# The first load of a half-rotary kernel in two transfers by partitions, 16 and 112

## The chip, the cores and the metric

The kernel runs on one core of a Trainium2 chip. Its time is the device time of one execution in microseconds (us), as the median of several runs; beside it stands one profiled execution, whose trace is read here. Of the core's engines only VectorE (DVE in the profile) computes. SyncE (SP) and GpSimd (POOL) issue transfers between the chip's memory (DRAM) and the on-chip memory, which has 128 partitions; sixteen DMA engines carry them out.

## The reference

`x` is 16 x 512 x 16 x 64 (batch, sequence, heads, dim), `cos` and `sin` are 512 x 32. Only the first half of the last axis is rotated, in two quarters of 16 elements; the second half, `x2`, is passed on.

```python
half_dim = dim // 2
x1, x2 = (x[..., :half_dim].copy(), x[..., half_dim:].copy())
cos = cos[None, :, None, :].copy()
sin = sin[None, :, None, :].copy()
rotated_first = x1[..., :half_dim // 2] * cos[..., :half_dim // 2] - x1[..., half_dim // 2:] * sin[..., :half_dim // 2]
rotated_second = x1[..., :half_dim // 2] * sin[..., :half_dim // 2] + x1[..., half_dim // 2:] * cos[..., :half_dim // 2]
return np.concatenate([rotated_first, rotated_second, x2], axis=-1).astype(np.float32)
```

## The kernel before

The 8192 positions (batch times sequence) are cut into T = 4 tiles of 128 partitions by K = 16 consecutive positions. One position is 16 heads x 64 floats, so a partition's row of a tile is 64 KB in one contiguous piece of DRAM, and a tile is 8.39 MB. The tiles live in `ring`, which has NS = 3 slots: tile 3 takes the slot of tile 0. A tile is loaded, rotated in place, and stored from the same bytes, so that the second half of each vector needs no work.

Two helpers issue the large transfers: `load(t, lo, hi)` on SP's queue (line 55) and `store(t, lo, hi, queue)`, on SP's queue unless told otherwise (line 58). A transfer moves positions lo to hi of all 128 partitions of a tile; the first half of a tile (0 to KC = 8) is 32 KB a partition.

`cos` and `sin` go by two small transfers on GpSimd's queue (lines 63 and 64) into every fourth partition of `stage`. VectorE spreads them over all partitions with a shuffle (line 73), four copies into `packed` (line 80) and four into `table` (line 83).

`rotate(t, lo, hi)` is four VectorE instructions over positions lo to hi of a tile: two products, the first into `b_t` in the accumulation memory (line 96) and the second in place (line 97), a difference (line 98) and a sum (line 101).

The order of the work is the order in the code on each engine's queue. SP issues load(0), load(1), load(2, 0, KC), then store(0) when tile 0 is rotated, the second half of load(2), load(3) when store(0) has landed (it needs the slot), store(1), and store(3) at the end; store(2) goes by GpSimd's queue. A dependency written out by hand (lines 118 to 123) holds store(1) back until positions 8 to 13 of tile 2 are rotated.

Any instruction that reads what a transfer wrote waits for that transfer's completion. The first `rotate(0, 0, KC)` reads all 128 partitions of slot 0.

Of the kernel before, what the change touches and what calls it, by code (L numbers as in the profile page):

```python
# [1 line left out]

# [4 lines left out]


@with_exitstack
def kernel(  # L10
    ctx: ExitStack,
    tc: tile.TileContext,
    x: bass.AP,
    cos: bass.AP,
    sin: bass.AP,
    out: bass.AP,
):
    nc = tc.nc
    fp32 = mybir.dt.float32
    P = 128  # L20
    B, S, H, D = x.shape
    Q = D // 4
    HF = D // 2

    K = 16
    T = B * S // (P * K)
    PB = S // K
    REP = P // PB  # L30
    R = H * D
    NS = 3
    KC = K // 2
    KM = 13

    xf = x.rearrange("b s h d -> (b s h d)").rearrange("(t p f) -> t p f", t=T, p=P)
    of = out.rearrange("b s h d -> (b s h d)").rearrange("(t p f) -> t p f", t=T, p=P)
    cosf = cos.rearrange("(p k) j -> p (k j)", k=K)
    sinf = sin.rearrange("(p k) j -> p (k j)", k=K)

    const_pool = ctx.enter_context(tc.tile_pool(name="const", bufs=1))
    b_pool = ctx.enter_context(tc.tile_pool(name="bp", bufs=1, space=bass.MemoryType.PSUM))


    ring = const_pool.tile([P, NS, K, H, D], fp32)
    stage = const_pool.tile([P, 2, K, HF], fp32)
    spun = const_pool.tile([P, 2 * K, Q], fp32)
    packed = const_pool.tile([PB, 2 * K, Q], fp32)
    table = const_pool.tile([P, 2, K, 2, Q], fp32)

    def rows(t, lo, hi):
        return ring[:, t % NS, lo:hi].rearrange("p k h d -> p (k h d)")

    def load(t, lo=0, hi=K):
        return nc.sync.dma_start(out=rows(t, lo, hi), in_=xf[t, :, lo * R : hi * R])

    def store(t, lo=0, hi=K, queue=nc.sync):
        return queue.dma_start(out=of[t, :, lo * R : hi * R], in_=rows(t, lo, hi))  # L58


    nc.vector.memset(stage[:, :, :, 0:Q], 0.0)  # L61
    spread = stage.rearrange("(j b) t k i -> j b t (k i)", b=REP)
    nc.gpsimd.dma_start(out=spread[:, 0, 0], in_=cosf)  # L63
    nc.gpsimd.dma_start(out=spread[:, 0, 1], in_=sinf)  # L64
    load(0)
    load(1)
    load(2, 0, KC)

    PQ = PB // REP
    nc.vector.stream_shuffle(  # L73
        out=spun[:],
        in_=stage.rearrange("p t k j -> p (t k) j")[:, :, 0:Q],
        mask=[j % PQ * REP for j in range(PB)],
    )
    for q in reversed(range(REP)):
        n = PQ * (q + 1)
        nc.vector.tensor_copy(out=packed[0:n], in_=spun[q * PB : q * PB + n])  # L80

    for r in range(REP):
        nc.vector.tensor_copy(  # L83
            out=table[r * PB : (r + 1) * PB].rearrange("p t k c j -> p (t k) c j"),
            in_=packed.unsqueeze(2).to_broadcast((PB, 2 * K, 2, Q)),
        )
    C = table[:, 0].rearrange("p k c j -> p k (c j)")
    Sn = table[:, 1].rearrange("p k c j -> p k (c j)")

    def rotate(t, lo, hi):  # L90
        x1 = ring[:, t % NS, lo:hi, :, 0:HF]
        c = C[:, lo:hi].unsqueeze(2).to_broadcast((P, hi - lo, H, HF))
        s = Sn[:, lo:hi].unsqueeze(2).to_broadcast((P, hi - lo, H, HF))
        b_full = b_pool.tile([P, KC, H, HF], fp32, name="b_t")
        b_t = b_full[:, 0 : hi - lo]
        nc.vector.tensor_mul(out=b_t, in0=x1, in1=s)  # L96
        nc.vector.tensor_mul(out=x1, in0=x1, in1=c)  # L97
        nc.vector.tensor_sub(  # L98
            out=x1[:, :, :, 0:Q], in0=x1[:, :, :, 0:Q], in1=b_t[:, :, :, Q:HF]
        )  # L100
        return nc.vector.tensor_add(  # L101
            out=x1[:, :, :, Q:HF], in0=x1[:, :, :, Q:HF], in1=b_t[:, :, :, 0:Q]
        )

    rotate(0, 0, KC)
    rotate(0, KC, K)
    store(0)
    load(2, KC, K)
    load(3)
    rotate(1, 0, KC)  # L110
    rotate(1, KC, K)
    behind_loads = store(1)
    rotate(2, 0, KC)
    near = rotate(2, KC, KM)
    rotate(2, KM, K)
    store(2, queue=nc.gpsimd)

    tc.add_manual_dep(
        behind_loads.ins,
        near.ins.name,  # L120
        mybir.DependencyInfo(mybir.DependencyClass.Sync, mybir.DependencyReason.DATA),
        reason="the store follows the loads at the DMA engines",
    )
    rotate(3, 0, KC)
    rotate(3, KC, K)
    store(3)


# [1 line left out]
_INS = ['x', 'cos', 'sin']  # L130
_OUTS = [((16, 512, 16, 64), 'float32')]


# [23 lines left out]
```

## Time and profile before

| | |
|---|---|
| median of 3 runs | 161.42 us (161.4 to 161.52) |
| profiled execution, span from first to last instruction | 159.5 us |
| VectorE busy | 112.9 us |
| bytes read and written in DRAM | 33.69 MB and 33.55 MB |
| mean rate over the span | 422 GB/s |
| load(0), load(1), load(2, 0, KC) issued | from 0.74 us, 1.33 us for the three |
| first `rotate` starts | 22.99 us |
| last `rotate` ends, store(3) issued | 131.2 us |

The span is shorter than the time of a run by 1.9 us, which lie around the instructions. The profile shows the instructions of each engine and, apart from them, the packets of the DMA engines. The instruction that issues a transfer is short (0.34 to 0.64 us here); the transfer lands much later, and the profile gives the time from issue to landing on its own. "q1" is the queue that SP's transfers use, "q0" that of GpSimd's.

Two views matter most below. The strip of the span in 40 slices shows which engine is busy when:

```profile
DVE  1000959999999999999999999999999990000000
POOL 3000000000000000000000000010000000000000
DMA  7969979899699699699996996996996996998966
```

Each digit is the busy share of a slice of 4 us in tenths. VectorE is idle for the first 16 us but for a little, and again behind 131 us; the DMA digits go up and down because a packet is booked in one slice and a full row lasts more than half of one.

The other is the waits of SP's queue, which say what the issue of a transfer stood for:

```profile
SPq L58 <- DVE ring L101: 84.1, 3, 30.5
SPq L152 <- DMA out_dram<-ring: 26.8, 2, 14.4
SPq L58 <- DMA ring<-in_x_dram: 22.3, 2, 20.8
SPq L55 <- DMA out_dram<-ring: 21.0, 1, 21.0
```

The columns are the waiting line and what it waited for, then the total in us, the number of times and the longest. The last row is load(3), which waits 21 us for store(0) to leave its slot.

### The profile page before, as it was taken

The numbers are of one execution on the slowest core, as the hardware profiler recorded it, in microseconds if no ns is written. First come the engines' busy times: TensorE is split into PE (matmuls) and PEld (weight loads), VectorE is DVE, ScalarE is ACT, GpSimd is POOL, SyncE is SP. The second block draws the span as 40 slices with busy tenths as digits, with TensorE's granted clock in tenths as the row PEclk, the third lists the DMA queues.
The fourth block names the chain that finished last, engine by engine and source line by source line (L and its number), as shares of the span: only waits on it lengthen the run. The fifth ranks groups of instructions, "written<-read, shape, count | busy, mean of one in ns | idle before, by whom it ended". The sixth has DMA issues, their size and how long they took to land.

```text
span 159.5 us, 115 instructions
## 1 busy us (share of the span) xinstructions
DVE 112.9 (71%) x47; POOL 1.9 (1%) x7
## 2 busy tenths in 40 slices
DVE  1000959999999999999999999999999990000000
POOL 3000000000000000000000000010000000000000
DMA  7969979899699699699996996996996996998966
GB/s 263 542 263 542 444 345 526 362 427 526 271 493 551 263 526 526 263 395 427 493 526 263 526 526 263 526 526 263 526 526 263 526 510 279 526 427 362 526 263 263
DMA packets 1360, 67.24 MB, mean 422 GB/s; under 512 B 176, under 2 KB 176, under 8 KB 208
## 3 DMA queue, kind: packets, MB, share of 16 engines
q1 hardware_dynamic: 1152, 58.72, 85.7%
q0 software_dynamic: 208, 8.52, 12.4%
HBM read 33.69 MB, written 33.55 MB: 422 GB/s over the span
## 4 chain that ended last, share of the span: by engine, by line
DVE 61%; DMA 14%; issue 5%; DVEq 1%
DVE b_t L96 22%; DVE ring L97 22%; DMA ring<-in_x_dram 14%; DVE ring L101 10%; DVE ring L98 7%; DVEq L152 1%; DVEq L96 0%
## 5 line engine op out<-in xcount | busy, mean ns | idle before, releaser
L96 DVE TENSOR_TENSOR b_t<-ring,table 128x4096 f32<-128x4096 f32 (+2 forms) x9 | 35.6, 3959 | 2.1 <-DMA ring<-in_x_dram 1.9
L97 DVE TENSOR_TENSOR ring<-ring,table 128x4096 f32<-128x4096 f32 (+2 forms) x9 | 35.6, 3950 | 0.3
L98 DVE TENSOR_TENSOR ring<-ring,b_t 128x2048 f32<-128x2048 f32 (+2 forms) x9 | 18.4, 2050 | 0.3
L101 DVE TENSOR_TENSOR ring<-ring,b_t 128x2048 f32<-128x2048 f32 (+2 forms) x9 | 18.4, 2043 | 0.0
L73 DVE LOAD_MASK_SELECT spun<-stage x1 | 0.0, 14 | 14.4 <-DMA stage<-in_sin_dram 14.4
L83 DVE COPY table<-packed 32x1024 f32<-32x1024 f32 x4 | 2.7, 684 | 0.1
L58 POOL DMA_DIRECT2D out_dram<-ring x1 | 0.6, 559 | 101.7 <-DVE ring L101 101.7
L80 DVE COPY packed<-spun 32x512 f32<-32x512 f32 (+3 forms) x4 | 1.7, 416 | 0.1
L61 DVE MEMSET stage<- 128x512 f32 x1 | 0.5, 485 | 0.9 <-PEq L141 0.9
L73 DVE STREAM_SHUFFLE spun<-stage 128x512 f32<-128x512 f32 x1 | 0.7, 722 | 0.0
L63 POOL DMA_DIRECT2D stage<-in_cos_dram x1 | 0.6, 642 | 1.3 <-DVE stage L61 1.3
L64 POOL DMA_DIRECT2D stage<-in_sin_dram x1 | 0.5, 532 | 0.0
L141 POOL MEMSET const-bfloat16-1.0<- 128x1 bf16 x1 | 0.1, 101 | 0.0
L141 POOL MEMSET const-float32-0.0<- 128x1 f32 x1 | 0.1, 98 | 0.2 <-issue 0.2
L141 POOL MEMSET const-float32-1.0<- 128x1 f32 x1 | 0.1, 98 | 0.0
L141 POOL MEMSET const-uint8-127<- 128x1 uint8 x1 | 0.1, 98 | 0.0
## 6 DMA issues: line engine op xcount, KB each, us to landing
ring<-in_x_dram SPq DMA_DIRECT2D x2, 4096.0 KB, 40.7
stage<-in_cos_dram POOLq DMA_DIRECT2D x1, 64.0 KB, 8.9
stage<-in_sin_dram POOLq DMA_DIRECT2D x1, 64.0 KB, 13.3
ring<-in_x_dram SPq DMA_DIRECT2D x3, 28.9
out_dram<-ring SPq DMA_DIRECT2D x3, 27.4
out_dram<-ring POOLq DMA_DIRECT2D x1, 39.5
```

The source lines that it names most:

```text
L58: return queue.dma_start(out=of[t, :, lo * R : hi * R], in_=rows(t, lo, hi))
L61: nc.vector.memset(stage[:, :, :, 0:Q], 0.0)
L63: nc.gpsimd.dma_start(out=spread[:, 0, 0], in_=cosf)
L64: nc.gpsimd.dma_start(out=spread[:, 0, 1], in_=sinf)
L73: nc.vector.stream_shuffle(out=spun[:], in_=stage.rearrange("p t k j -> p (t k) j")[:, :, 0:Q], mask=[j % PQ * REP for j in range(PB)],)
L80: nc.vector.tensor_copy(out=packed[0:n], in_=spun[q * PB : q * PB + n])
L83: nc.vector.tensor_copy(out=table[r * PB : (r + 1) * PB].rearrange("p t k c j -> p (t k) c j"), in_=packed.unsqueeze(2).to_broadcast((PB, ...
L96: nc.vector.tensor_mul(out=b_t, in0=x1, in1=s)
L97: nc.vector.tensor_mul(out=x1, in0=x1, in1=c)
L98: nc.vector.tensor_sub(out=x1[:, :, :, 0:Q], in0=x1[:, :, :, 0:Q], in1=b_t[:, :, :, Q:HF])
L101: return nc.vector.tensor_add(out=x1[:, :, :, Q:HF], in0=x1[:, :, :, Q:HF], in1=b_t[:, :, :, 0:Q])
L152: with _tile.TileContext(nc) as tc:
```

## The change

The call `load(0)` is replaced by a loop over two ranges of partitions, 0 to 15 and 16 to 127. Each pass issues one transfer on SP's queue, of the same 64 KB rows from and to the same places. The other transfers and all of VectorE's work are as before; one transfer more is issued, and `rotate(0, 0, KC)` now reads what two transfers wrote.

```diff
     KC = K // 2
     KM = 13
+    FIRST = 16
...
     nc.gpsimd.dma_start(out=spread[:, 0, 0], in_=cosf)
     nc.gpsimd.dma_start(out=spread[:, 0, 1], in_=sinf)
-    load(0)
+    for lo, hi in ((0, FIRST), (FIRST, P)):
+        nc.sync.dma_start(
+            out=ring[lo:hi, 0].rearrange("p k h d -> p (k h d)"), in_=xf[0, lo:hi]
+        )
     load(1)
     load(2, 0, KC)
```

## The prediction

> **What bounds the kernel now.** I began with the head of the page and its table of queues, to see whether an engine or the transfers fill the span.
>
> ```profile
> span 159.5 us, 115 instructions
> DVE 112.9 (71%) x47; POOL 1.9 (1%) x7
> ...
> DMA packets 1360, 67.24 MB, mean 422 GB/s; under 512 B 176, under 2 KB 176, under 8 KB 208
> ...
> q1 hardware_dynamic: 1152, 58.72, 85.7%
> q0 software_dynamic: 208, 8.52, 12.4%
> ```
>
> The two queues together use 85.7 + 12.4 = 98.1% of sixteen engines' time; VectorE (DVE) is busy for 71%. The packet counts say how a transfer is cut. Queue q1 carries eight transfers of 128 rows: 8 x 128 = 1024, and 1152 - 1024 = 128 = 8 x 16. The kernel has eleven transfers in all, and 11 x 16 = 176 packets lie under 512 B. So each row of a partition is one packet, and each transfer closes with sixteen tiny ones, one per engine.
>
> Next, the transfers over time, by stretches: the columns are the stretch, its length, busy VectorE and GpSimd, the clock, the share of the DMA engines and GB/s. A packet is booked where it starts, so short stretches can exceed 1.
>
> ```profile
> 0.00:20.00 20.00, 4.50 (x10) 1.37 (x6) 1.00 0.99 413
> 20.00:40.00 20.00, 18.03 (x7) 0.00 (x0) 1.00 1.00 433
> ...
> 22.00:23.00 1.00, 0.01 (x1) 0.00 (x0) 1.00 2.43 1049
> 23.00:24.00 1.00, 1.00 (x1) 0.00 (x0) 1.00 0.00 0
> 24.00:25.00 1.00, 1.00 (x1) 0.00 (x0) 1.00 2.42 1049
> ```
>
> The engines have no gap in the load stage. In the stretch from 24 to 25 us 1.049 MB start, which is 16 x 65,536 bytes, one full row on each engine, and the share of 2.42 is their mean length: 2.42 us. I call this a turn. A tile of 128 full rows is 8 turns, 19.4 us. That all sixteen keep 2.42 us while all work is shown only for transfers over all 128 partitions.
>
> Then the chain that ended last, and the waits.
>
> ```profile
> 0.74 22.16 DMA ring<-in_x_dram
> ...
> 22.99 4.44 DVE b_t L96
> 27.43 0.02 issue
> 27.46 4.43 DVE ring L97
> ...
> 128.97 2.20 DVEq L152
> ```
>
> ```profile
> DVE spun L73 <- DMA stage<-in_sin_dram: 14.4, 1, 14.4
> DVE b_t L96 <- DMA ring<-in_x_dram: 1.9, 1, 1.9
> ```
>
> The chain begins with the very transfer that is split: load(0) lands at 0.74 + 22.16 = 22.9 us, VectorE starts L96 at 22.99 and never stops until 131.2 us. The tables were ready earlier: the last copy on L83 ends 1.85 us before. What follows 131.2 is store(3).
>
> ```profile
> 131.19 0.34 SPq L58 DMA_DIRECT2D out_dram<-ring  x1
> ```
> ```profile
> q1 hardware_dynamic: 160, 8.39, 68.0%
> q0 software_dynamic: 64, 3.15, 25.5%
> ```
>
> The second pair is the queue table for 131 to 159.5 us: beside the 8.39 MB of store(3), 3.15 MB of store(2) are still being written, 25.5% of 28.5 us = 7.3 us. So two things end together: VectorE's chain, started by load(0), and the transfer engines' backlog. Delay only VectorE and up to 7.3 us vanish in that backlog; delay both and the whole delay shows.
>
> **The change, part by part.**
>
> *One more issue on SP.* The three L55 issues at the start take 1.33 us together, 0.44 each. load(1) and load(2, 0, KC) go out 0.44 us later, behind 8 turns of queued rows: nothing. Without that cover it would cost 0.44 us. The cos and sin transfers are on the GpSimd queue and are not passed. VectorE's first multiplication waits for one more completion: the chain's row for such a step (DVEq L96, 0.02 us) prices it; nothing else on VectorE is late by more.
>
> *Sixteen more tiny packets.* From 0 to 22.5 us the GpSimd queue's 64 packets, half of them 4 KB, took 1.5% of sixteen engines: 0.015 x 22.5 x 16 / 64 = 0.084 us each. One more per engine: at most 0.08 us, on the path.
>
> *A first transfer with sixteen rows.* As a tile of 128 rows gives 8 to each engine, 16 rows should give one. If each still takes 2.42 us, this part costs 0. But the sixteen rows are an eighth of the partitions, and nothing in the trace shows sixteen engines writing into so few. If the rate falls with the share of partitions, the part takes 8 turns, 19.4 us: +16.9. A gain is bounded by the start: the old issue took 0.44 us, and if a smaller transfer lets the first packets go sooner, it is by less than that. Between +16.9 and -0.44 I take 4 turns, the middle in whole turns: 3 x 2.42 = +7.3 us. The nearest row, the full tile, is 8 times as wide, so it doesn't decide.
>
> [...]
>
> *A second transfer with 112 rows.* Seven rows for each engine. With no collisions: 7 turns, as before, +0. If every row met another engine on its way in, each turn would take twice as long: 14 turns, +16.9. That 128 rows in eights run without hindrance need not carry over to 112 in sevens; and engines that get ahead start load(1)'s rows while others are behind. I take the middle, 10.5 turns: 3.5 x 2.42 = +8.5 us. Below nothing has no reason: 7 rows at 2.42 us is the full speed shown.
>
> *Where the stall goes.* load(0) lands at 22.9 + 7.3 + 8.5 + 0.1 = 38.8 us. cos and sin queue behind the first rows: 15.8 us becomes 23.1 at worst, the tables (last copy ends at 18.36 + 2.78 = 21.1) become 28.4; 10 us of cover remain. VectorE's wait before L96 grows from 1.9 to some 17.7 us, and its chain ends at 147.0. The transfers are late alike, because the rows behind load(0) are on the same engines: store(0), issued at 49.9 us today, meets the end of the first three loads (the last was issued at about 1.6 us and landed 50.3 later, at 52) in the same relation. So the backlog at the end absorbs nothing.
>
> *Sum.* 159.5 + 7.3 + 8.5 + 0.1 = 175.4 us of span. The median of the runs, 161.42, is 1.9 above the profiled span, so 177.3 us.
>
> **The rivals.**
>
> *Only the first part is slow.* The 112 rows run clean, the loss is 7.3 + 0.1: 168.8 us; with 3 turns instead of 4, 166.3. For it: the larger transfer covers seven eighths of the partitions, as today's loads cover all. Against: nothing shows its rows dealt out without overlap.
>
> *Nothing happens.* Every row takes 2.42 us wherever it lands: +0.1, 161.5 us. For it: the engines keep 2.42 us through loads. Against: all those were full tiles.
>
> *The other side, faster.* With full speed per row, a smaller first transfer may start the engines sooner. Its place is the head of the chain, where 1 us passes between the issue at 0.74 us and the first packets (the stretch from 1 to 2 us is the first that moves bytes); its price is at most one issue, -0.44 + 0.08 = -0.36, so 161.1 us. It decides only if the first part takes one turn. The tables allow it: 1.85 us of slack.
>
> *Both parts crowd.* If the 112 rows are dealt so that sixteen neighbours are always written together, all 8 turns take four times as long: 8 x 7.3 = +58, 220 us; between this and the forecast lies everything over 182.
>
> **How the numbers follow.** Forecast (a slow first part, collisions in the second): 54%, its own range 173 to 182. Only the first part: 27%, 166.3 to 173. Nothing: 7%. Faster: 4%. Crowded beyond 182: 8%. The range goes from 166.3 (3 turns, no collisions) to 182.1 (6 turns, +12.1, and the collisions at +8.5), which leaves out 19%. About 0.2%, 0.32 us, is what this kernel's runs tell from no change. Faster 0.04, same 0.07, slower 0.89.
>
> **What would show it.** In the changed profile: VectorE's wait before the first multiplication near 17.7 us (9.2 if only the first part is slow, 1.9 if nothing is); the first stretches with 1.049 MB starting, then some 10 us before the next full rows start; transfer-engine time above 100% of what the bytes need at 2.42 us per row, in the first 40 us only; tables done by 28.4 us; VectorE gapless behind its first start; the tail after it unchanged at 28.3 us. The forecast falls if rows of the first transfer take 2.42 us, or if the tail shrinks by several us, which would mean the engines caught up while VectorE did not.

## The result, and the profile after

The changed kernel takes 183.87 us (median of 5 runs, 183.46 to 184.14) against 161.42 us of the kernel before: 22.45 us more, a ratio of 1.138 with a 95% interval of 1.137 to 1.140. The forecast was slower, 177.3 us with a range to 182.1; the time lies 1.8 us above that range.

The head of the changed kernel's page and its queue table:

```profile
span 181.5 us, 116 instructions
...
DVE 112.9 (62%) x47; POOL 1.9 (1%) x7
...
q1 hardware_dynamic: 1168, 58.72, 86.6%
q0 software_dynamic: 208, 8.52, 11.0%
```

VectorE does the same 112.9 us of work, the bytes are the same, and there are the sixteen further packets. The two queues together still keep the sixteen engines busy for 97.6% of a span that is 22 us longer. So the engines hardly idled more; the same bytes took longer. Where, the chain of the changed kernel shows (start in us, length, what):

```profile
1.19 43.54 DMA ring<-in_x_dram
...
44.84 4.44 DVE b_t L100
```

The second of the two transfers is issued at 1.19 us and lands at 44.7, where load(0) had landed at 22.9. VectorE starts 21.85 us later than before, and from there everything has its old distance: store(3) goes out at 153.04 us, 28.5 us before the end (28.3 before). The waits on VectorE:

```profile
DVE spun L77 <- DMA stage<-in_sin_dram: 29.3, 1, 29.3
DVE b_t L100 <- DMA ring<-in_x_dram: 8.8, 1, 8.8
```

The wait for `sin` has doubled from 14.4 to 29.3 us. The tables are ready at 44.84 - 8.8 = 36.0 us, and still before the rows of tile 0.

The rows of the first load, by stretches of the changed kernel (start and end, length, VectorE, GpSimd, clock, share of the DMA engines, GB/s; packets are booked where they start):

```profile
1.00:2.00 1.00, 0.40 (x1) 0.29 (x1) 1.00 5.93 721
2.00:3.00 1.00, 0.00 (x0) 0.88 (x2) 1.00 2.66 328
...
9.00:12.00 3.00, 0.00 (x0) 0.00 (x0) 1.00 1.78 350
15.00:17.00 2.00, 0.00 (x0) 0.00 (x0) 1.00 2.49 557
20.00:22.00 2.00, 0.00 (x0) 0.00 (x0) 1.00 1.64 524
23.00:26.00 3.00, 0.00 (x0) 0.00 (x0) 1.00 1.17 326
27.00:30.00 3.00, 0.00 (x0) 0.00 (x0) 1.00 1.50 350
31.00:35.00 4.00, 3.80 (x8) 0.00 (x0) 1.00 1.17 262
36.00:40.00 4.00, 0.09 (x1) 0.00 (x0) 1.00 1.13 262
```

A stretch in which 16 rows start (GB/s times length near 1.05 MB) gives their mean length as share times length. The first two lines together are the sixteen rows of the first transfer: 5.93 + 2.66 = 8.6 us on average, not 2.42. Then come the seven rounds of rows of the second transfer (a round is one row on each engine): 1.78 x 3 = 5.3 us, some 4.7 (4.98 with the small packets of `cos` in it), 1.64 x 2 = 3.3, some 3.8 (1.17 x 3 x 16 / 15, as 326 GB/s are fifteen rows), 1.50 x 3 = 4.5, 1.17 x 4 = 4.7 and 1.13 x 4 = 4.5. Both transfers are slow, and the second costs more. The first one's rows last 8.6 - 2.42 = 6.2 us longer than a turn; of the 21.85 us by which VectorE is late, the other 15.6 belong to the second. Its seven rounds add up to 30.8 us, 13.9 more than 7 x 2.42; the remaining 1.8 us go with rows that no longer start together, as those of the last round start between 36.6 and 39.0 us and the transfer has landed only with the last of them.

### The profile page after: what moved, and what is told of

Its sections match the earlier page's. It is cut to its first block, busy times and chain, and to the rows that moved or that the text cites. A ratio compares the mean times of both kernels' runs of the same rounds, so it can differ in the third digit from the quotient of the medians.

```text
span 181.5 us, 116 instructions
## 1 busy us (share of the span) xinstructions
DVE 112.9 (62%) x47; POOL 1.9 (1%) x7
## 4 chain that ended last, share of the span: by engine, by line
DVE 54%; DMA 24%; issue 4%; DVEq 1%; SPq 0%
DMA ring<-in_x_dram 24%; DVE b_t L100 20%; DVE ring L101 20%; DVE ring L105 9%; DVE ring L102 6%; DVEq L156 1%; SPq L67 0%; DVEq L100 0%
## 5 line engine op out<-in xcount | busy, mean ns | idle before, releaser
L77 DVE LOAD_MASK_SELECT spun<-stage x1 | 0.0, 14 | 29.3 <-DMA stage<-in_sin_dram 29.3
## 6 DMA issues: line engine op xcount, KB each, us to landing
stage<-in_sin_dram POOLq DMA_DIRECT2D x1, 64.0 KB, 28.3
```

What stands on the lines that cost most here:

```text
L77: nc.vector.stream_shuffle(out=spun[:], in_=stage.rearrange("p t k j -> p (t k) j")[:, :, 0:Q], mask=[j % PQ * REP for j in range(PB)],)
```

## The experiments

"Place" below is the theory that the time of a row depends on which partitions are being written at the same moment: partitions that share a "way in" would be written one after the other. Engines "meet" when their rows go to one way in at the same time. Which partitions share one was the author's assumption in every expectation below, and so was each number of ways in; no trace shows a way in, the traces show how long the rows took. The rivals are that a further transfer costs by itself, or that the number of rows does.

**Two transfers over all partitions.**

```diff
-    load(0)
+    load(0, 0, 2)
+    load(0, 2, K)
     load(1)
```

> The first load in two transfers again, but cut by positions: 8 KB of every partition, then 56 KB, over all 128 partitions. If the loss comes from which partitions a transfer covers (place), this costs one issue behind cover and sixteen tiny packets: 161.3 to 161.8 us, and VectorE's wait before its first product stays at 1.9 us. If it comes from having two transfers and two completions on the head of the chain (rival), most of the 22.5 us is still there: above 175 us.

Measured: 161.64 us, ratio 1.0003 (0.9986 to 1.0021). The wait before the first product is 3.1 us and not 1.9, because the tables were ready earlier: `sin` was waited for 13.1 us where it was 14.4 before. A second transfer with a second completion costs nothing that can be seen here; the partitions remain.

**One transfer more, to price a shape by itself.** The next kernels keep load(0) whole and repeat some rows of tile 0 behind it, into the slot that tile 2 overwrites later. The output stays the same; the time holds the extra bytes. It holds a second thing, too: load(2, 0, KC) writes the same slot and waits for the extra rows, and SP's later transfers go out behind it (SP waits 53.6 us there with the 112 rows below). The engines had other rows to move meanwhile: from 20 to 160 us their share is 1.00 in the kernels with ranges 0 to 63, 32 to 95, 0 to 15 and 16 to 127. So the length of the rows is the first reading in what follows, and the total the second. Only the range differs:

```diff
     load(0)
+    nc.sync.dma_start(
+        out=ring[0:64, 2].rearrange("p k h d -> p (k h d)"), in_=xf[0, 0:64]
+    )
     load(1)
```

> One transfer more, behind load(0): partitions 0 to 63 of tile 0 once more, into the slot of tile 2 that is loaded later anyway; four full rows for each engine. [...] Place theory: two engines share each way in, a row takes 4.8 us instead of 2.42, the extra transfer takes 4 x 4.84 = 19.4 us and the total is about 180.8 us. Rival (only the number of rows or of transfers counts): 4 x 2.42 = 9.7 us at full speed, 171.1 us, or whatever the next kernel, with the same number of rows, shows.

The other has `32:96` in both places.

> The same extra transfer of 64 rows, of partitions 32 to 95. [...] Place theory: every row at 2.42 us, 9.7 us more, 171.1 us, some 9.7 us under the kernel with partitions 0 to 63. Rival (number of rows, or of partitions missing): no difference between the two.

Measured: 182.34 us (ratio 1.129, 1.126 to 1.131) with partitions 0 to 63, 172.63 us (1.068, 1.066 to 1.069) with 32 to 95. A stretch in which extra rows start, first of the kernel with 0 to 63:

```profile
26.00:28.00 2.00, 1.97 (x2) 0.00 (x0) 1.00 2.56 524
```

and of the kernel with 32 to 95:

```profile
26.00:28.00 2.00, 1.97 (x2) 0.00 (x0) 1.00 1.21 524
```

In both, 524 GB/s over 2 us are sixteen rows. They take 2.56 x 2 = 5.1 us in the one and 1.21 x 2 = 2.42 us in the other. Same queue, same number of rows, same bytes, same distance of the rows in DRAM: only the partitions differ, and with them the rows' addresses in DRAM, by 2 MB. Both rivals fall here. What no run separates is the partition from the address of its row in DRAM, since the extra rows always go to the partitions that they have in tile 0. That two engines share a way in with partitions 0 to 63 was not shown; the times that the theory took from it, 4.84 us a row and 2.42 us with 32 to 95, agree with the traces but for 0.3 us a row.

**The sixteen rows alone**, `0:16`, and sixteen rows spread out, `0:128:8`.

> One transfer more behind load(0): partitions 0 to 15 of tile 0 once more, into the slot of tile 2. Place theory: four engines share each way in, a row takes four turns, 9.7 us, total 171.1 us. If sixteen rows run at full speed: 2.4 us, 163.9 us. If the rate falls with the share of partitions (an eighth): 19.4 us, 180.8 us.

> One transfer more behind load(0), sixteen rows again, but of every eighth partition (0, 8, ... 120). [...] Rival (the number of rows sets the rate): the same total as with partitions 0 to 15.

Measured: 171.80 us (1.062, 1.060 to 1.064) and 167.59 us (1.036, 1.034 to 1.039). The stretch in which the sixteen rows start, with neighbours

```profile
22.00:24.00 2.00, 0.00 (x0) 0.00 (x0) 1.00 4.27 524
```

and with every eighth partition

```profile
22.00:24.00 2.00, 0.00 (x0) 0.00 (x0) 1.00 2.30 492
```

4.27 x 2 = 8.5 us against 2.30 x 2 x 16 / 15 = 4.9 us (492 GB/s are fifteen rows). The transfer of neighbours adds 171.80 - 161.65 = 10.15 us, four turns of 2.42 and a little, of which 2.42 us are its bytes: the loss is 7.7 us. With strided rows VectorE's first product waited for the extra transfer too (it starts at 28.8 us there, at 24.33 with neighbours), here and in the strided kernels below, so the total is not the transfer's price alone; the length of its rows is the reading.

**The 112 rows alone**, `16:128`.

> One transfer more behind load(0): partitions 16 to 127 of tile 0 once more, seven full rows for each engine, in the steady flow and with no sixteen-row transfer before it. In the changed kernel these rows took about 4.3 us each. If the slow rows are the second transfer's own: some 30 us more, about 192 us, with rows near 4.6 us and a faster stretch in the middle where fewer engines meet. If they were an after-effect of the crowded sixteen rows ahead of them: 7 x 2.42 = 17 us, 178.4 us. If only the engines that meet on a way in are slow (two pairs of sixteen): between, about 183 us, most rows at 2.42 us.

Measured: 194.11 us (1.200, 1.198 to 1.202), 32.46 us more. At full speed 7 x 2.42 = 16.9 us would be its bytes; the loss is 15.5 us. The rows are slow without any sixteen rows ahead of them, so they are no after-effect. Its stretches:

```profile
22.00:24.00 2.00, 0.08 (x1) 0.00 (x0) 1.00 2.18 524
...
26.00:28.00 2.00, 2.00 (x1) 0.00 (x0) 1.00 2.38 524
...
30.00:32.00 2.00, 2.00 (x1) 0.00 (x0) 1.00 1.52 492
...
33.00:36.00 3.00, 3.00 (x2) 0.00 (x0) 1.00 1.20 306
```

The first round of rows takes 4.4 us, the second 4.8, the third 1.52 x 2 x 16 / 15 = 3.2, the fourth 1.20 x 3 x 16 / 14 = 4.1 (306 GB/s are fourteen rows): the fast stretch in the middle is there too, as in the changed kernel. Which engines meet in which round no run shows, and why the third round is faster than the others was not followed. There is a surprise besides: in the second round all sixteen rows are slow, at 4.7 to 4.8 us in the trace, where the last case of the expectation had two slow pairs and the other rows at 2.42 us.

**Who pays for a meeting?** Single rows behind load(0), while the engines that have none go on with load(1). The ranges were `0:2` (called one pair), `0:8:2` (two pairs), `0:16:4` (four rows apart), `0:4` (four on one way in), `0:128:32` (two pairs far apart); the names in brackets go by the author's assumption. These kernels and the three after them ran once each, so their totals have no interval.

> One transfer more behind load(0): partitions 0 and 1 alone, so two engines on one way in, while the other fourteen go on with load(1). Place theory: these two rows take 4.8 us. If a crowded way in also holds up the others, the fourteen rows of load(1) that run beside them take longer than 2.42 us; if not, they keep 2.42 us. Total 161.4 to 166.3 us.

The four extra rows of partitions 0, 2, 4 and 6, taken as two pairs:

> [...] Place theory: these rows take 4.8 us. The twelve others, at load(1): 2.42 us if only those that meet are slow; near 4.6 us if two crowded ways in slow everybody, as the rows of the changed kernel's second transfer suggest. Total about 166.3 us in both cases, since the slowest engine sets it.

Those of partitions 0, 4, 8 and 12, four apart:

> [...] In the kernel with two pairs all sixteen rows that ran beside each other took 4.0 to 4.8 us. If crowding did that: here every row keeps 2.42 us, total 163.9 us. If any extra transfer on four engines does it: again 4.0 to 4.8 us for all, total 166.3 us.

> Partitions 0 to 3: four engines on one way in. The four rows should take 9.7 us, total 171.1 us. The twelve others, at load(1): 2.42 us if one crowded way in never holds up others, as beside one pair; well over 2.42 us if it takes three or four engines that are held up, however many ways in they crowd.

Those of partitions 0, 32, 64 and 96, taken as two pairs again:

> [...] The pairs' rows: 4.8 us, total 166.3 us. If two held-up pairs slow the twelve others wherever they lie: 4.0 to 4.8 us for all sixteen. [...]

The same stretch, in which sixteen rows start, the extra ones among them. One pair:

```profile
22.00:24.00 2.00, 0.86 (x1) 0.00 (x0) 1.00 1.33 524
```

Two pairs:

```profile
22.00:24.00 2.00, 0.00 (x0) 0.00 (x0) 1.00 2.20 524
```

Four rows apart:

```profile
22.00:24.00 2.00, 0.00 (x0) 0.00 (x0) 1.00 1.21 524
```

Four on one way in:

```profile
22.00:24.00 2.00, 0.67 (x1) 0.00 (x0) 1.00 4.17 524
```

Four rows 32 apart:

```profile
22.00:24.00 2.00, 0.00 (x0) 0.00 (x0) 1.00 2.59 524
```

Each share times 2 is the mean of sixteen rows. Apart: 2.42 us, all at full speed, so four extra rows do no harm by themselves. One pair: 2.66 us; the trace has the packets one by one, and they are fourteen rows of 2.42 and two of 4.2 and 4.3. Two pairs: 4.40 us; if only the four were slow, at 4.84, the mean would be (12 x 2.42 + 4 x 4.84) / 16 = 3.0. Four on one way in: 8.34 us; if only the four were slow, at 9.7, it would be 4.2. In the trace, all sixteen rows take 4.0 to 4.8 us in the one and 7.5 to 9.1 us in the other. So the twelve others, rows of load(1), took about as long as the four extra ones. The totals of one pair, two pairs, four apart and four on one were 166.72, 166.61, 164.07 and 171.16 us. With rows 32 apart all were slow again, a mean of 2.59 x 2 = 5.2 us: thirteen rows of 4.6 to 5.0 us and three of 6.4 to 7.4. The total was 168.80 us, 2.5 above what was expected for pairs.

Then three rows on one way in (`0:3`), three apart (`0:12:4`), and one row in each half (`0:128:64`):

> Partitions 0, 1 and 2 once more behind load(0): three engines on one way in, so 3 x 2.42 = 7.3 us for these rows, total 166.3 us. If everybody is held up as soon as two engines have to stand back: the other thirteen take 6 to 7.3 us too. If it takes four engines in two pairs or more: the thirteen keep 2.42 us.

> Partitions 0, 4 and 8: three rows on three ways in. All rows 2.42 us, total 163.9 us. If an extra transfer on three engines slows the others by itself, they are slow here too and the crowd is not the cause.

The rows of partitions 0 and 64, one in each half of the 128:

> [...] If the halves are separate, both rows take 2.42 us, total 163.9 us. If they share something, as the 6.4 to 7.3 us of the rows 32 apart suggest, these two take longer than 2.42 us, up to 4.8 us and 166.3 us.

Three on one way in, and one row in each half:

```profile
21.90:24.00 2.10, 0.92 (x1) 0.00 (x0) 1.00 1.66 499
```

```profile
22.00:24.00 2.00, 0.00 (x0) 0.00 (x0) 1.00 1.32 524
```

Three on one: a mean of 1.66 x 2.1 = 3.5 us, in the trace three rows of 6.2 to 7.0 us, near the 7.3 that were expected, and thirteen of 2.7 to 2.8: touched, not stopped. So the second of the two expectations is nearly met. Its total, 168.66 us, is 2.4 above the 166.3 written there, but that figure does not follow from the rows: 161.4 + 7.3 = 168.7, which is what was measured. Three apart: 163.86 us, as expected. So the two rows of partitions 0 and 1 pay alone (4.2 and 4.3 us beside 2.42), the three of 0 to 2 nearly so, and with four extra rows all sixteen paid, but for the rows four apart.

The row in each half came out at 166.27 us with a mean of 2.64 us, in the trace two slow rows of 4.2 among fourteen of 2.42. That is what was expected if the halves share something, but it need not be the reason: the fourteen others are rows of load(1), which the expectation had left out of account, and whether the two rows slowed each other or were slowed by rows of load(1) no run shows.

**The first load in three transfers.**

```diff
-    load(0)
+    for lo, hi in ((32, 96), (0, 32), (96, P)):
+        nc.sync.dma_start(
+            out=ring[lo:hi, 0].rearrange("p k h d -> p (k h d)"), in_=xf[0, lo:hi]
+        )
```

> The first load in three transfers by partitions: 32 to 95, 0 to 31, 96 to 127, nothing loaded twice. Place theory, from the runs so far: 32 to 95 at 2.42 us a row (4 turns), the two others on 8 ways in each, 5.1 us a row as with partitions 0 to 63, two rows an engine: 9.7 + 4 x 5.1 = 30.2 us against 19.4, so about 172.2 us. Rival (each further transfer by partitions costs as the changed kernel's did): at least its 183.9 us.

Measured: 174.52 us, ratio 1.082 (1.079 to 1.085). One transfer more than in the changed kernel, and 9.3 us faster. It is 2.3 us above the expectation: the last piece lands at 34.3 us (its chain piece is 2.00 + 32.28), 11.4 after load(0)'s 22.9 where 10.8 were expected; what makes up the rest was not followed. The 8 ways in of the two outer pieces were not shown either; a stretch in which rows of the last piece start has a share of 2.56 over 2 us, 5.1 us a row, as the expectation took. No version tried was faster than the kernel before.

## Why the prediction was wrong, point by point

*What bounds the kernel.* Right. Transfers and VectorE's chain were late together, the tail stayed (28.5 us for 28.3), and the span grew by 22.0 us for a start 21.85 us later. Nothing vanished in the backlog.

*One more issue, sixteen tiny packets, one more wait.* Right: the cut by positions has all of them and costs nothing that can be seen.

*A first transfer with sixteen rows.* Right that it is slow, and right in size: 4 turns and +7.3 us were taken; its rows lose 6.2 us in the changed kernel, and the transfer 7.7 us by itself. The size was partly luck. It was the middle between two bounds, not worked out from who meets whom.

*A second transfer with 112 rows.* This is the step that failed: "I take the middle, 10.5 turns: 3.5 x 2.42 = +8.5 us." It measured 32.46 us by itself, 13.4 turns, a loss of 15.5 us, and in the changed kernel it has 15.6 us of VectorE's delay. That is close to the bound of 14 turns that was named for "if every row met another engine on its way in". The middle was taken without a row that speaks for it, and the working had engines that "get ahead" while others are behind. The runs show that the others don't get ahead: with the rows of partitions 0, 2, 4 and 6 among them all sixteen rows took 4.0 to 4.8 us, and in the second round of the 112 rows all took 4.7 to 4.8. So four crowded rows cost a round nearly the 4.84 us that the bound takes for meetings everywhere. With the two losses measured, 161.42 + 7.7 + 15.5 + 0.1 = 184.7 us, 0.8 above the result.

*The range.* It went to 182.1 us by crowding the first part further while it held the second at its middle. The second part's own bound with the first as taken, 161.4 + 7.3 + 16.9 + 0.1 = 185.7 us, would have held the time. As it was, the time fell among the 8% for "crowded beyond 182", for a reason other than the one given there.

*Where the stall goes.* Partly wrong. The tables were to be done by 28.4 us "at worst", with 10 us of cover; they were done at 36.0, with 8.8. The `cos` and `sin` packets lie between the rows, and the rows of the second transfer were slow as well, which this step left out: the first small packets start at 7.2 us before and at 15.1 after, the last at 12.7 and at 26.0. It cost nothing, because tile 0 came later still; but for that reason VectorE's wait before its first product was 8.8 us and not the 17.7 that the prediction named as its sign. That sign did not fit its own working either: with load(0) at 38.8 and the tables at 28.4 us the wait is 10.4 us.

*The rivals.* "Nothing happens" and the faster case fall with a first row of 8.6 us. "Only the first part is slow" falls with the 112 rows. "Both parts crowd", with turns four times as long, 9.7 us, falls with rounds of 3.3 to 5.3 us.

*The sums of the experiments.* Two engines to a way in stand behind the 180.8 us expected with partitions 0 to 63, four behind the 171.1 us with 0 to 15, and two pairs behind the 166.3 us with 0, 2, 4 and 6 and with rows 32 apart. No run shows these terms; the runs showed mean rows of 5.1, 8.5, 4.4 and 5.2 us, and totals of 182.34, 171.80, 166.61 and 168.80 us.

## What to carry to other kernels

Cut a transfer by positions, along the axis that lies within a partition, and not along the partitions: the same number of transfers cost nothing in the one case and 22 us in the other. If a cut along partitions must be, price the piece by which partitions are written at the same moment, not by its bytes, and count four crowded rows as a loss for all engines of that round: here all sixteen rows took 4.0 to 4.8 us with partitions 0, 2, 4 and 6 among them and 7.5 to 9.1 us with 0 to 3, where 2.42 is full speed. An estimate of such a cost comes cheaply from one extra copy of the transfer in the steady flow, read off as the length of its rows: the two copies here add up to within 0.8 us of the changed kernel.

## What the runs showed of the hardware that was not expected

Four crowded rows held up the twelve beside them. Sixteen rows that started together took a mean of 4.4 us with partitions 0, 2, 4 and 6 among them and 8.3 us with 0 to 3, all of them slow, while the rows of 0 and 1 left the fourteen others at 2.42 us, and those of 0 to 2 left the thirteen others at 2.7 to 2.8. Which engines share a way in the traces don't show; they show the lengths. What is shared between them, and whether it matters that the extra rows of these kernels ran on few engines next to a full transfer, no run here tells.

A transfer of 64 rows took 2.42 us a row, full speed, with partitions 32 to 95, and 5.1 us with 0 to 63.
